# Attention forward on one core: the last head's two query halves in one PSUM tile or in two

## The chip, the cores and the metric

The kernel runs on one core of one Trainium2 chip. The metric is device microseconds of one execution. The kernel before takes 118.95 us, the median of three runs (118.91 to 118.98). One more execution was recorded by the profiler; its numbers are in the profile section below.

## The reference: what is computed

Softmax attention for 8 batches of 8 heads, 512 queries and 512 keys of 64 elements each, in float32, with no mask:

```python
def reference(q, k, v):
    scale = 1.0 / np.sqrt(q.shape[-1])
    scores = np.einsum('bhqd,bhkd->bhqk', q, k) * scale
    scores = scores - scores.max(axis=-1, keepdims=True)
    attn = np.exp(scores)
    attn = attn / attn.sum(axis=-1, keepdims=True)
    return np.einsum('bhqk,bhkd->bhqd', attn, v).astype(np.float32)
```

The kernel leaves the subtraction of the maximum out, since exp(x)/sum(exp(x)) is the same without it. It gets the sum of each row for nothing by giving V a 65th column of ones.

## The kernel before, in words

**Tiles.** The 64 heads are taken as 32 pairs (0 to 31). 512 queries and 512 keys are four chunks of 128 each. For every pair, q and k are cast to fp16 on GpSimd, transposed on TensorE into PSUM and copied to SBUF on VectorE. For every key chunk c and head h, TensorE then makes a block of scores with the 128 keys on the partitions and the 512 queries along the free dimension (L511). Two such blocks make a group, which fills one PSUM tile of the pool `ps_st`, tag `st`, of 128 x 2 x 512 float32. The pool holds three of these tiles and hands them out in turn: this is the score ring. One instruction on ScalarE exponentiates a whole group into an fp16 tile `pt` in SBUF (L516). Ten of the groups are exponentiated by VectorE instead (L533, L550).

**Values.** For one head and one chunk of 128 queries, four products (one for each key chunk c) accumulate 128 x 65 float32 in PSUM: `pt` is the stationary side and V with its ones column the moving side (L585). VectorE divides by the 65th column (L563, L565) into an SBUF ring, and SyncE stores a head when it is complete (L574).

**Who sets the order.** The class `Plan` steps through the kernel with costs written by hand and notes which step each engine takes next; the kernel then issues its instructions in that order. The engines wait for one another through semaphores, which a tile framework puts in by tile: an instruction that writes a tile waits for the earlier ones that read it, whichever part of the tile they touch.

**The last head.** The very last head (pair 31, h = 1) is not in the normal list (`Plan.last`). Its key chunks 0 and 1 are group 126. Its key chunks 2 and 3 are exponentiated in two half groups, 127 for queries 0 to 255 and 128 for queries 256 to 511 (`half` in `scores`, L489 to L517). So the last three tiles of the score ring are those of groups 126, 127 and 128. The values of this head are made by `last_values` in four parts (L593 to L609), from one more tile of the score ring, `o_last`, which follows group 128 and so takes the buffer of group 126:

- part 0: key chunk 0, all four query chunks (4 products), after the exponential of group 126
- part 1: key chunk 1, all four query chunks (4 products)
- part 2: key chunks 2 and 3, query chunks 0 and 1 (4 products), after the exponential of group 127
- part 3: key chunks 2 and 3, query chunks 2 and 3 (4 products), after the exponential of group 128

Query chunks 0 and 1 accumulate in `o[:, 0]`, query chunks 2 and 3 in `o[:, 1]` of the same tile. `finish` (L611 to L624) follows part 2 with the first half and part 3 with the second: a reciprocal on VectorE (L616), a multiplication on VectorE (L617), and a store of 64 KB, the first from SyncE's queue and the second from ScalarE's (L624).

In `Plan`, `wants` (L193) gives the exponential that each part needs, and `last_values` (L206) lets a part start when that exponential and the buffer are there.

Of the kernel before, what the change touches and what calls it, by code (L numbers as in the profile page):

```python
# [8 lines left out]
FP32 = mybir.dt.float32  # L9
# [8 lines left out]
class Plan:  # L18
# [174 lines left out]
    def wants(self, g, h, part):  # L193
        members = [self.member[(g, c, h)] for c in range(4)]
        if (g, h) == self.last:
            end = len(self.groups)
            members = [(members[0], members[1], end - 2, end - 1)[part]]
        exps = max(self.exps.get(m, 1e9) for m in members)
        return max(exps, self.cast_done.get((g, "v"), 1e9))

# [4 lines left out]

    def last_values(self, t):  # L206
        g, h = self.last
        if self.m < len(self.groups) or self.last_part == 4 or t < self.read[-3]:
            return False
        if t < self.wants(g, h, self.last_part):  # L210
            return False
        self.note(t, "last", self.last_part)
        self.full(t, self.V_UNIT)
        if self.last_part > 1:
            self.ready.append((self.pe + self.TO_DVE, "finish", (self.last_part,)))
        self.last_part += 1
        return True

# [124 lines left out]
def kernel(  # L343
# [7 lines left out]
    nc = tc.nc  # L351
    B, H, S, D = q.shape
    P = 128
    NI = S // P
# [4 lines left out]
    LAST = NP - 1  # L359
# [19 lines left out]
    opool = ctx.enter_context(tc.tile_pool(name="out", bufs=4))  # L379
    ps_st = ctx.enter_context(tc.tile_pool(name="ps_st", bufs=3, space=bass.MemoryType.PSUM))  # L380
# [16 lines left out]
    blocks = {}  # L397
# [4 lines left out]
    last = {}  # L402

    def source(src, g):
        b, h = g // ppb, 2 * (g % ppb)
        return src[b, h : h + 2].rearrange("h (p i) d -> p h i d", i=NI)
# [184 lines left out]
            )  # L591

    def last_values(part):  # L593
        if part == 0:
            o = ps_st.tile([P, 2, S], FP32, tag="st", name="o_last")
            last["o"] = [
                o[:, n, 0 : 2 * (D + 1)].rearrange("p (x d) -> p x d", x=2) for n in range(2)
            ]
        o = last["o"]
        for c in (part,) if part < 2 else (2, 3):  # L600
            for x in (range(NI), range(NI), (0, 1), (2, 3))[part]:
                nc.tensor.matmul(
                    o[x // 2][:, x % 2, :],
                    blocks[(LAST, c, 1)][:, x * P : (x + 1) * P],
                    vps[LAST % NV][:, 1, c, :],
                    start=(c == 0 and x % 2 == 0),
                    stop=(c == NI - 1),
                    skip_group_check=True,
                )  # L609

    def finish(part):  # L611
        o = last["o"][part - 2]
        n = slice(2 * part - 4, 2 * part - 2)
        ob = opool.tile([P, 2, D], FP32, tag="obl", name=f"obl_{part}")
        rc = opool.tile([P, 7, 1], FP32, tag="rc", name=f"rc_last_{part}")
        nc.vector.reciprocal(out=rc[:, 0:2], in_=o[:, :, D : D + 1])  # L616
        nc.vector.tensor_tensor(  # L617
            out=ob[:, :, :],
            in0=o[:, :, 0:D],
            in1=rc[:, 0:2].broadcast_to([P, 2, D]),  # L620
            op=AluOp.mult,
        )
        queue = (nc.sync, nc.scalar)[part - 2]
        queue.dma_start(out=source(out, LAST)[:, 1, n], in_=ob[:, :, :])  # L624

    def first_loads():
# [99 lines left out]
    with tc.manual_schedule():  # L726
        plan = Plan(groups, NP, 3)
        steps = plan.run()
        first_loads()
        for g, name in plan.first_loads:  # L730
            load(g, name)
        make_identity(nc, ident)
        nc.vector.memset(lift, LIFT[0])
        for p in (32, 96):
            nc.vector.memset(lift[p : p + 32], LIFT[1])
        for n in range(NV):
            nc.vector.memset(vps[n][:, :, :, D : D + 1], 1.0)
        first_pair()
        do = {
            "transposes": transposes,  # L740
            "scores": scores,
            "values": values,
            "load": load,
            "cast": cast_behind,
            "raise": raise_,
            "copy": lambda g, b: copy(g),
            "pass": pass_,
            "last": last_values,
            "finish": finish,
            "norm": lambda u, n, b: normalise(u, n),  # L750
        }
        for what, *args in steps:
            do[what](*args)
# [30 lines left out]
```

## Time and profile before

| what | value |
|---|---|
| three runs | 118.91, 118.95, 118.98 us |
| the profiled execution | 119.28 us |
| its span, first to last instruction | 117.5 us |
| outside the span (119.28 - 117.5) | 1.8 us |
| granted TensorE clock over the span | 1.000 |
| ScalarE busy | 110.7 us (94%), 123 instructions |
| TensorE busy | 105.0 us (89%), 1579 matmuls |
| VectorE busy | 98.2 us (84%), 174 instructions |
| 16 matmuls of the last head (L602) | 190 to 203 ns each, from 112.9 to 114.3 us |
| last reciprocals (L616), multiplications (L617) | 171 ns and 292 ns each, two of each |
| the two last stores (L624), issue to landing | 1.6 us each |

Times inside the profile are counted from the first instruction. The page gives for each engine its busy time, then the chain of work that ended last, then the costliest groups of instructions. The trace behind it answers with more: the chain in order of time, the instructions of an engine in order of time, the waits (who waited for whom, in total, times, longest), and the busy time of each engine in chosen stretches. "L602" is line 602 of the kernel; "PEld" is the load of the stationary side, "PE" the matmul itself, "q" behind an engine is its sequencer, which issues DMAs.

### The profile page before, as it was taken

The page shows a single profiled execution, that of the slowest core. Times are in us where ns is not written, and L with a number is a line of the kernel's source. Part 1 is how long each engine was busy: PE and PEld are TensorE (multiplying, and loading weights), DVE is VectorE, ACT ScalarE, POOL GpSimd, SP SyncE. Part 2 cuts the span into 40 slices and gives each one's busy share as a digit, 9 for nine tenths or more (in the row PEclk, how much of TensorE's full clock was granted, in tenths as well). Part 3 has the DMA queues.
Part 4 walks back from the last instruction along what each step waited for, and adds up shares of the span by engine and source line. Part 5 has one row for each costly group of instructions (what it writes and reads, how often), then busy time and mean ns, then how long its engine had stood idle before and what let it go on. Part 6 is the DMA issues. An engine that isn't in the chain of part 4 may idle for free.

```text
span 117.5 us, 4082 instructions
## 1 busy us (share of the span) xinstructions
PE 105.0 (89%) x1579; PEld 66.5 (57%) x1579; DVE 98.2 (84%) x174; ACT 110.7 (94%) x123; POOL 58.4 (50%) x102
## 2 busy tenths in 40 slices
PE   7969996987998999898997999999899998999970
PEld 2536653664655666355764575565566556666550
DVE  3463898699899999999999969899978999996371
ACT  4599999999999999999999999999999999999970
POOL 2388725944725843355583595569246553441000
PEclk9999999999999999999999999999999999999999
DMA  4999999999999999999899897999999993242353
GB/s 102 315 354 381 388 374 370 367 367 340 337 342 316 352 363 319 274 356 359 265 301 302 226 316 251 287 347 320 320 368 352 345 342 109 90 137 90 103 173 95
DMA packets 35604, 33.83 MB, mean 288 GB/s; under 512 B 2688, under 2 KB 35584, under 8 KB 35584
## 3 DMA queue, kind: packets, MB, share of 16 engines
q1 hardware_dynamic: 35152, 33.24, 86.0%
q10 hardware_dynamic: 432, 0.33, 0.9%
q8 instruction: 12, 0.20, 0.7%
q14 instruction: 8, 0.07, 0.2%
HBM read 25.17 MB, written 8.39 MB: 286 GB/s over the span
## 4 chain that ended last, share of the span: by engine, by line
ACT 44%; PE 24%; issue 12%; DVE 11%; POOL 3%; DMA 3%; SPq 1%; POOLq 0%; ACTq 0%
ACT pt L516 43%; PE st L511 8%; PE o L585 8%; DVE y L550 3%; PE st_0a L635 3%; DMA out_dram<-ring 3%; DVE z L533 2%; POOL qkp L445 2%; PE tp L469 2%; DVE ring L565 2%; DVE tqk L482 2%; DVE pd L550 1%; ACT pt L685 1%; PE st L678 1%; PE st L497 1%
## 5 line engine op out<-in xcount | busy, mean ns | idle before, releaser
L516 ACT ACTIVATE pt<-st 128x1024 f16<-128x1024 f32 (+1 forms) x116 | 105.7, 1293 | 0.0
L511 PE MATMUL st<-tqk 64*128 64x512 f16 (+1 forms) x250 | 45.6, 380 | 5.3 <-ACT pt L516 3.5
L585 PE MATMUL o<-vp,pt 128*128 128x65 f16 x928 | 42.3, 194 | 0.4 <-DVE tqk L482 0.2
L585 PEld LDWEIGHTS <-pt 128*128 128x128 f16 x928 | 35.6, 98 | 12.1 <-issue 10.9
L435 POOL CAST vp<-v 128x512 f16<-128x512 f32 x32 | 20.3, 640 | 16.4 <-DVE y L550 7.6
L445 POOL CAST qkp<-k 128x512 f16<-128x512 f32 x31 | 19.1, 615 | 14.7 <-DVE rc L563 2.6
L445 POOL CAST qkp<-q 128x512 f16<-128x512 f32 x30 | 18.5, 615 | 13.7 <-DVE pd L550 5.4
L565 DVE TENSOR_TENSOR ring<-o,rc 128x448 f32<-128x448 f32 (+2 forms) x37 | 22.6, 612 | 1.5 <-DVE rc L563 0.3
L511 PEld LDWEIGHTS <-tqk 64*128 64x128 f16 x250 | 13.1, 93 | 18.2 <-issue 10.4
L482 DVE COPY tqk<-tp 128x1024 f16<-128x1024 f16 x30 | 20.5, 684 | 1.0 <-PE tp L469 1.0
L469 PE MATMUL tp<-ident,qkp 128*128 128x128 f16 x248 | 19.6, 220 | 1.3 <-DVE tqk L482 0.6
L469 PEld LDWEIGHTS <-qkp 128*128 128x128 f16 x248 | 14.2, 97 | 9.5 <-issue 4.4
L533 DVE TENSOR_SCALAR z<-st 128x1024 f32<-128x1024 f32 x10 | 12.2, 1221 | 2.5 <-PE st L511 2.3
L563 DVE RECIPROCAL rc<-o 128x7 f32<-128x7 f32 (+2 forms) x37 | 7.4, 200 | 6.9 <-PE o L585 6.5
L550 DVE SCALAR_TENSOR_TENSOR y<-y 128x1024 f32<-128x1024 f32 x10 | 12.4, 1240 | 0.0
L550 DVE SCALAR_TENSOR_TENSOR y<-z 128x1024 f32<-128x1024 uint16 x10 | 12.3, 1234 | 0.1
L550 DVE SCALAR_TENSOR_TENSOR pd<-y,z 128x1024 uint32<-128x1024 f32 x10 | 12.2, 1217 | 0.0
L585 PE MATMUL o<-vp,pd 128*128 128x65 f16 x80 | 11.8, 195 | 0.0
L585 PEld LDWEIGHTS <-pd 128*128 128x128 f16 x80 | 7.8, 98 | 1.5 <-issue 0.8
L497 PE MATMUL st<-const-bfloat16-1.0,lift 64*128 64x512 bf16 x20 | 3.9, 380 | 0.8 <-ACT pt L516 0.6
L635 PE MATMUL st_0a<-const-bfloat16-1.0 128*128 128x512 bf16 (+1 forms) x11 | 3.5, 484 | 0.8 <-PEq L768 0.8
L635 PEld LDWEIGHTS <-const-bfloat16-1.0 128*128 128x128 bf16 x15 | 1.7, 131 | 2.4 <-issue 2.4
(48 smaller groups left out, 22.5 us busy)
## 6 DMA issues: line engine op xcount, KB each, us to landing
out_dram<-ring SPq DMA_DIRECT2D x63, 128.0 KB, 4.1
k<-in_k_dram SPq DMA_DIRECT2D x31, 256.0 KB, 5.1
q<-in_q_dram SPq DMA_DIRECT2D x31, 256.0 KB, 5.0
v<-in_v_dram SPq DMA_DIRECT2D x27, 256.0 KB, 5.0
v<-in_v_dram SPq DMA_DIRECT2D x10, 128.0 KB, 4.2
k<-in_k_dram ACTq DMA_DIRECT2D x2, 128.0 KB, 2.8
q<-in_q_dram SPq DMA_DIRECT2D x2, 128.0 KB, 2.7
out_dram<-obl SPq DMA_DIRECT2D x1, 64.0 KB, 1.6
```

Of the source, the lines that this page charges most:

```text
L435: return nc.gpsimd.tensor_copy(out=vps[g % NV][:, :, :, 0:D], in_=raw[g]["v"][:, :, :, :])
L445: return nc.gpsimd.tensor_copy(out=dst, in_=src[:, :, :, :])
L469: nc.tensor.transpose(tps[g][:, n, i, :], qkp[g][:, n, i, :], ident)
L482: nc.vector.tensor_copy(out=tqk[g][:, :, :], in_=tps.pop(g).rearrange("p n i c -> p n (i c)"))
L511: nc.tensor.matmul(st[:, x, cols], kc, qc[:, cols], start=not on_dve, stop=True)
L516: nc.scalar.activation(out=pt[:, :, cols], in_=st[:, :, cols], func=EXP, scale=scale)
L533: nc.vector.tensor_scalar(out=r["z"][:, :, :], in0=r["st"][:, :, :], scalar1=STEP, scalar2=2.0**17, op0=AluOp.mult, op1=AluOp.max,)
L550: nc.vector.scalar_tensor_tensor(out=r["bits"][:, :, :] if last else r["y"][:, :, :], in0=r["y"][:, :, :] if s else f, scalar=QUARTIC[s], ...
L563: nc.vector.reciprocal(out=rc[:, 0:n], in_=o[:, x : x + n, D : D + 1])
L565: nc.vector.tensor_tensor(out=ring[:, u % NU : u % NU + n, :], in0=o[:, x : x + n, 0:D], in1=rc[:, 0:n].broadcast_to([P, n, D]), op=AluOp. ...
L585: nc.tensor.matmul(os[u // 7][:, u % 7, :], blocks[(g, c, h)][:, y * P : (y + 1) * P], vps[g % NV][:, h, c, :], start=(c == 0), stop=(c == ...
L635: nc.tensor.matmul(dst[:, 0:n], ones[:, 0:P], ones[:, 0:n], start=True, stop=True)
```

## The change

The last head's two query halves get a tile of the score ring each, `o_last0` and `o_last1`, instead of two regions of one tile. Each tile is allocated when its half begins, so `o_last0` takes the buffer of group 126 and `o_last1` that of group 127. The four parts are now:

- part 0: key chunks 0 and 1, query chunks 0 and 1 (4 products), after the exponential of group 126
- part 1: key chunks 2 and 3, query chunks 0 and 1 (4 products), after that of group 127; the first `finish` follows
- part 2: key chunks 0 and 1, query chunks 2 and 3 (4 products), into the second tile
- part 3: key chunks 2 and 3, query chunks 2 and 3 (4 products), after the exponential of group 128; the second `finish` follows

The sixteen products, the reciprocals, multiplications and stores are the same instructions as before. The diff, cut to its core:

```diff
@@ Plan.wants
-            members = [(members[0], members[1], end - 2, end - 1)[part]]
+            members = [(members[1], end - 2, members[1], end - 1)[part]]
@@ Plan.last_values
-        if self.m < len(self.groups) or self.last_part == 4 or t < self.read[-3]:
+        if self.m < len(self.groups) or self.last_part == 4:
             return False
-        if t < self.wants(g, h, self.last_part):
+        if t < max(self.wants(g, h, self.last_part), self.read[self.last_part // 2 - 3]):
             return False
...
-        if self.last_part > 1:
-            self.ready.append((self.pe + self.TO_DVE, "finish", (self.last_part,)))
+        if self.last_part % 2:
+            self.ready.append((self.pe + self.TO_DVE, "finish", (self.last_part // 2,)))
@@ last_values
-        if part == 0:
-            o = ps_st.tile([P, 2, S], FP32, tag="st", name="o_last")
-            last["o"] = [
-                o[:, n, 0 : 2 * (D + 1)].rearrange("p (x d) -> p x d", x=2) for n in range(2)
-            ]
-        o = last["o"]
-        for c in (part,) if part < 2 else (2, 3):
-            for x in (range(NI), range(NI), (0, 1), (2, 3))[part]:
+        half, second = divmod(part, 2)
+        if not second:
+            o = ps_st.tile([P, 2, S], FP32, tag="st", name=f"o_last{half}")
+            last[half] = o[:, 0, 0 : 2 * (D + 1)].rearrange("p (x d) -> p x d", x=2)
+        for c in (2 * second, 2 * second + 1):
+            for x in range(2):
+                y = 2 * half + x
                 nc.tensor.matmul(
-                    o[x // 2][:, x % 2, :],
-                    blocks[(LAST, c, 1)][:, x * P : (x + 1) * P],
+                    last[half][:, x, :],
+                    blocks[(LAST, c, 1)][:, y * P : (y + 1) * P],
                     vps[LAST % NV][:, 1, c, :],
-                    start=(c == 0 and x % 2 == 0),
+                    start=(c == 0 and x == 0),
@@ finish
-    def finish(part):
-        o = last["o"][part - 2]
-        n = slice(2 * part - 4, 2 * part - 2)
+    def finish(half):
+        o = last[half]
+        n = slice(2 * half, 2 * half + 2)
...
-        queue = (nc.sync, nc.scalar)[part - 2]
+        queue = (nc.sync, nc.scalar)[half]
```

More of the change, by code (lines that the diff above doesn't have):

```diff
@@ L609, in last_values @@
                 )
-    def finish(part):
-        o = last["o"][part - 2]
-        n = slice(2 * part - 4, 2 * part - 2)
-        ob = opool.tile([P, 2, D], FP32, tag="obl", name=f"obl_{part}")
-        rc = opool.tile([P, 7, 1], FP32, tag="rc", name=f"rc_last_{part}")
+    def finish(half):
+        o = last[half]
+        n = slice(2 * half, 2 * half + 2)
+        ob = opool.tile([P, 2, D], FP32, tag="obl", name=f"obl_{half}")
+        rc = opool.tile([P, 7, 1], FP32, tag="rc", name=f"rc_last_{half}")
         nc.vector.reciprocal(out=rc[:, 0:2], in_=o[:, :, D : D + 1])
```

## The prediction, as it was put on record before the result

> **What bounds the kernel now.** First view: the page's opening line and, from its chain of work that ended last, the shares of the span by engine.
>
> ```profile
> span 117.5 us, 4082 instructions
> ...
> ACT 44%; PE 24%; issue 12%; DVE 11%; POOL 3%; DMA 3%; SPq 1%; POOLq 0%; ACTq 0%
> ```
>
> ScalarE has the largest share of the chain and is busy for 110.7 us: its exponentials set the pace up to the last of them. The change leaves them alone: in the two built programs every engine's instructions follow each other in the same order up to the sixteen products of the last head, and on ScalarE, VectorE, GpSimd and SyncE to the end. So only what comes after the last exponentials can move, and the second view is the chain in order of time over the last 5 us (start, length, what).
>
> ```profile
> 113.36 0.31 PE o_last L602 x4
> 113.68 0.02 issue
> 113.70 0.18 DVE rc_last L616
> 113.88 0.02 issue
> 113.91 0.30 DVE obl L617
> 114.21 0.04 issue
> 114.25 0.30 PE o_last L602 x4
> 114.55 0.02 issue
> 114.57 0.18 DVE rc_last L616
> 114.75 0.02 issue
> 114.78 0.29 DVE obl L617
> ```
>
> Read it as a zigzag. The exponential of group 127 ends at 113.31 and stands just ahead of these lines. Then come four products (part 2), the first half's reciprocal and multiplication on VectorE, and only then the last four products (part 3) and the second half's VectorE work. The exponential of group 128 is not in this chain: ScalarE's timeline has the last three exponentials end at 113.80 (111.30 + 2.50). The third view, the waits of the last microseconds (in total, times, longest), names what holds part 3.
>
> ```profile
> PE o_last L602 <- DVE obl L617: 0.6, 1, 0.6
> ```
>
> The fourth, the timeline, shows the same wait at the instructions, and the stores that close the kernel.
>
> ```profile
> 113.85 0.10 PEld L602 LDWEIGHTS <-pt 128*128 128x128 f16 x1 [0.31 <-ACT pt L516]
> ...
> 114.25 0.28 PE L602 MATMUL o_last<-vp,pt 128*128 128x65 f16 x4 [0.59 <-DVE obl L617]
> 114.26 0.40 SPq L624 DMA_DIRECT2D out_dram<-obl  x1
> ...
> 115.10 0.35 ACTq L624 DMA_DIRECT2D out_dram<-obl  x1
> ```
>
> The weights of part 3's first product were loaded at 113.85, 0.05 after the exponential of group 128; the product itself stood until 114.25, because it writes the tile that L617 was still reading. The two touch different columns of that tile; it is one tile in the program, and that is all that binds them. The last store (ScalarE's queue) is issued at 115.10, 0.03 after the last multiplication, and lands 1.55 later, at 116.65 (the trace's landing time); 0.84 of closing work follows to the end of the span.
>
> **The change, part by part.**
>
> *The wait that goes.* With two tiles part 3 no longer waits for L617. In the changed program its first product has no wait on VectorE left, and its first weight load still waits for the exponential of group 128. So part 3 starts at 113.85. Its length comes from the same four products after the other exponential: from the weight load at 113.36 to the reciprocal at 113.70 is 0.34. The second reciprocal can then start at 113.85 + 0.34 = 114.19 instead of 114.57: **0.38 earlier**.
>
> *What is late next.* VectorE must be free: the first multiplication runs from 113.91 to 114.20. In this trace an instruction of VectorE follows the one before it at anything from 0.08 before its reported end (wait met early, as in most of the L550 and L482 pairs) to 0.04 after it (the L616 to L617 step above). That puts the second reciprocal between 114.12 and 114.24; the products allow 114.19. So the gain lies between 0.33 (114.24) and 0.38, and I take 0.38, since a wait met by 114.19 is met before 114.20. The Trainium skill (VectorE: DVE Perf Modes, The DRAIN you can't avoid) says that the next instruction does not start until the pipe is empty; by that the start would be 114.20 and the gain 0.37. The overlaps of 0.08 in this trace speak against it.
>
> *The products that move.* Four products (key chunks 0 and 1, queries 256 to 511) go from before the exponential of group 127, where TensorE sat idle until 113.36, to right after part 1. Eight products issued together took 0.42 (112.87 to 113.29) against 0.30 for four, so they add 0.12 and are issued by about 113.63. Part 3 is due at 113.85: 0.22 to spare, cost nothing. If that cover were gone, part 3 would be late by at most 0.12. The first half (part 1) has the same four products behind the same exponential as before, so the first reciprocal stays at 113.70 and SyncE's store at 114.26.
>
> *The waits that come.* The second tile takes the buffer of group 127, which the exponential of group 127 reads. That exponential (ended 113.31) is what part 1 waits for anyway. The first product of part 2 gets one wait in the built program, on TensorE's own count up to the scores of group 127, which were made at 111.77 to 112.16: met long before. Should it nevertheless wait for part 1's products to be written (113.66, plus the 0.04 that a reciprocal needs behind them), part 2 would issue from 113.70 to 113.83, still before 113.85. So 0 to 0, and queued behind it is part 3 alone.
>
> *The last store.* VectorE's two instructions and the steps between them took 115.10 - 114.57 = 0.53 to the issue; so ScalarE's store is issued at 114.19 + 0.53 = 114.72. ScalarE has nothing else queued there. SyncE's issue lasts from 114.26 to 114.66, 0.06 before. What the 16 DMA engines do then is in the fifth view, stretches of the last 2 us (length, engines, clock, DMA share, GB/s).
>
> ```profile
> 115.25:115.53 0.28, 0.00 (x0) 0.00 (x0) 0.00 (x0) 0.00 (x0) 0.00 (x0) 1.00 0.65 185
> 115.53:115.95 0.42, 0.00 (x0) 0.00 (x0) 0.00 (x0) 0.00 (x0) 0.00 (x0) 1.00 0.00 0
> 115.95:116.32 0.37, 0.00 (x0) 0.00 (x0) 0.00 (x0) 0.00 (x0) 0.00 (x0) 1.00 0.61 177
> ```
>
> SyncE's store ends by 115.53, then the engines idle 0.42, then the last store runs 0.37. Moved by 0.38, the last store begins at 115.57, just behind. If it were to queue strictly behind SyncE's it could not begin before 115.53, so the gap caps any gain at 0.42.
>
> *Sum.* 0.38, from 119.28 to 118.90 for the profiled execution. Applied to the median of the runs shown, which is 0.33 below the profiled one: 118.95 - 0.38 = **118.57 us**. What the measurement of this kernel can tell from no change is about 0.2%, here 0.24.
>
> **The rivals.**
>
> *A. The second tile comes free only with the exponential of group 128.* Then eight products follow 113.85 instead of four: 0.12 later, gain 0.26, 118.69. Against it: the changed program has no such wait, and the buffers of the ring follow each other. Chance 0.07.
>
> *B. The two last stores get in each other's way.* They are now issued 0.06 apart instead of 0.44. SyncE's stores of 128 KB just before, each queued behind another, landed 1.8 to 1.9 after their issue instead of 1.55. With 1.86 the gain falls to 0.38 - 0.31 = 0.07: 118.88, within 0.2%. Against it: the transfers themselves do not overlap by the view above. The Trainium skill (Perfetto Trace Analysis, DMA Instruction — HWDGE) says that a sequencer locks the descriptor generator for its own use while it issues; by that ScalarE's issue would wait until 114.66, which is before 114.72, and nothing is lost. Chance 0.06.
>
> *C. The change does not do what it says,* or the end hangs on something else than this chain: 118.95. For it: 94% of the span is ScalarE's. Against it: SyncE's final wait ends 0.02 after the last store lands and nothing else is left. Chance 0.07.
>
> *D, slower: the last store meets a load of instructions.* The two stores that SyncE issued from 109.01 on (L574) landed 2.5 after their issue although the DMA engines were busy for 0.20 of 109 to 110; in that stretch the trace has single packets of the instruction queues, 8 to 16 KB, that hold one engine for 0.5 to 1.1. If the last store drew one, it would land after about 2.45, and the end would move by -0.38 + (2.45 - 1.55) = +0.52: 119.47. It turns into a loss where the landing takes over 1.55 + 0.38 = 1.93. Against it: the last such packet ends at 110.63, and the changed program has as many instructions as this one. Chance 0.06.
>
> **How the numbers follow.** The forecast has 0.74, A 0.07, B 0.06, C 0.07, D 0.06. Forecast and A are faster by over 0.2%: 0.81. B and C are the same: 0.13. D is slower: 0.06. The range: the largest gain is the 0.42 of the stores' gap (118.53), the smallest with the forecast and A is 0.26 (118.69); the runs spread by 0.07 and two medians are compared, so 0.08 below and 0.11 above: 118.45 to 118.80. It holds the forecast and A, 0.81.
>
> **What would show it.** Right: no wait of L601's products on L616 (the new numbers of these lines), part 3 issued at 0.05 after the last exponential, the second reciprocal starting within 0.05 of the end of the first multiplication, VectorE with no gap in its last four instructions after 113.70, ScalarE's store 0.38 earlier against the last exponential, and landing 1.55 after its issue. Wrong: a gap between the first multiplication and the second reciprocal (A), a landing over 1.7 (B, D), or a last exponential that itself ends elsewhere than 113.80, which nothing in the change explains.

## The result, and the profile after

The changed kernel takes 118.62 us against 119.12 us, medians of 22 runs each: ratio 0.996, 95% interval 0.9946 to 0.9973, which is 0.32 to 0.64 us less. The runs are much wider apart than the three shown before the prediction (118.91 to 118.98): 118.50 to 119.63 for the kernel before, 118.12 to 119.17 for the changed one. Two further measurements of the changed kernel gave 0.9989 and 0.9952 (below). All runs of both kernels together, 41 and 110, have means of 118.68 and 119.09: 0.42 less, with a 95% interval of 0.32 to 0.52. The 110 include 35 from a series that has no run of the changed kernel; the other series, each compared within itself and weighted by its runs, give 0.39.

The profiled execution took 118.68 us, with a span of 116.9. Its chain of work that ended last, in order of time (start, length, what), has lost the zigzag:

```profile
113.16 0.31 PE o_last L601 x4
113.47 0.02 issue
113.49 0.18 DVE rc_last L615
113.67 0.02 issue
113.70 0.29 DVE obl L616
113.99 0.18 DVE rc_last L615
114.17 0.02 issue
114.19 0.29 DVE obl L616
```

The second reciprocal now follows the first multiplication without a step back to TensorE. The waits of the last microseconds (in total, times, longest) no longer have a wait for that multiplication; what is left before the last head's products is a wait for exponentials:

```profile
PEld L601 <- ACT pt L516: 0.5, 2, 0.3
DVE rc L563 <- PE o L585: 0.3, 1, 0.3
PE o_last L601 <- ACT pt L516: 0.2, 1, 0.2
```

And the timeline shows the last exponential, the products and the stores:

```profile
112.55 1.05 ACT L516 ACTIVATE pt<-st 128x512 f16<-128x512 f32 x1
...
113.64 0.18 PEld L601 LDWEIGHTS <-pt 128*128 128x128 f16 x4 [0.19 <-ACT pt L516]
113.70 0.29 DVE L616 TENSOR_TENSOR obl<-o_last,rc_last 128x128 f32<-128x128 f32 x1
113.98 0.17 DVE L615 RECIPROCAL rc_last<-o_last 128x2 f32<-128x2 f32 x1
114.05 0.40 SPq L623 DMA_DIRECT2D out_dram<-obl  x1
...
114.51 0.35 ACTq L623 DMA_DIRECT2D out_dram<-obl  x1
```

The weights of part 3 are now loaded four in a row at 113.64, where the kernel before loaded one and stood.

The spans of the two profiled executions differ by 0.6, and that is not the gain. The last exponential ended at 113.59 in this execution (112.55 and 1.05 long, with rounding) and at 113.80 in the execution before:

```profile
112.75 1.05 ACT L516 ACTIVATE pt<-st 128x512 f16<-128x512 f32 x1
```

That 0.21 lies ahead of anything that the change touches: 0.09 of it is there at the first exponential, and the rest builds up evenly over the kernel. In the eleven profiled executions of this study the last exponential ended anywhere from 113.32 to 114.25. So the tail is read from the end of the last exponential, and every run below is read so, too:

| from the end of the last exponential, us | before | after |
|---|---|---|
| first reciprocal starts | -0.10 | -0.10 |
| first multiplication ends | 0.40 | 0.40 |
| part 3's first product starts | 0.45 | 0.06 |
| second reciprocal starts | 0.77 | 0.39 |
| last store issued | 1.30 | 0.92 |
| last store landed | 2.85 | 2.47 |
| end of the span | 3.69 | 3.31 |

0.38 is gained in one place, at part 3's start (0.39) and the second reciprocal's (0.38), and is carried unchanged to the end. The packets of the last store begin 0.06 after the last of SyncE's and take 0.36 (stretches: length, engines, clock, DMA share, GB/s):

```profile
115.31:115.37 0.06, 0.00 (x0) 0.00 (x0) 0.00 (x0) 0.00 (x0) 0.00 (x0) 1.00 0.03 9
115.37:115.73 0.36, 0.00 (x0) 0.00 (x0) 0.00 (x0) 0.00 (x0) 0.00 (x0) 1.00 0.62 181
```

### The profile page after: what moved, and what is told of

It reads as the page before. It is cut to its first block, busy times and chain, and to the rows that moved or that the text cites. A ratio compares the mean times of both kernels' runs of the same rounds, so it can differ in the third digit from the quotient of the medians.

```text
span 116.9 us, 4082 instructions
## 1 busy us (share of the span) xinstructions
PE 105.0 (90%) x1579; PEld 66.4 (57%) x1579; DVE 98.1 (84%) x174; ACT 110.6 (95%) x123; POOL 57.9 (50%) x102
## 4 chain that ended last, share of the span: by engine, by line
ACT 52%; PE 25%; DVE 11%; issue 9%; ACTq 0%
ACT pt L516 50%; PE st L511 9%; PE o L585 9%; DVE y L550 3%; PE st_0a L634 3%; PE tp L469 2%; ACT pt L684 2%; DVE z L533 2%; DVE tqk L482 2%; DVE ring L565 2%; DVE pd L550 1%; PE st L497 1%; DVE rc L563 1%; DVE obl L616 0%; DVE rc_last L615 0%
## 5 line engine op out<-in xcount | busy, mean ns | idle before, releaser
L435 POOL CAST vp<-v 128x512 f16<-128x512 f32 x32 | 19.6, 616 | 15.4 <-DVE y L550 7.6
```

Of the source, the lines that this page charges most:

```text
L435: return nc.gpsimd.tensor_copy(out=vps[g % NV][:, :, :, 0:D], in_=raw[g]["v"][:, :, :, :])
```

## The experiments

Theory W is the prediction's: what cost the time was part 3's wait for the first half's multiplication, and nothing else of the change matters. Rival O puts the gain down to the new order of the products, rival P to the two separate buffers.

### Two tiles and the new order, with the wait put back

```diff
@@ last_values
-                nc.tensor.matmul(
+                product = nc.tensor.matmul(
...
+                if (part, c, x) == (3, 2, 0):
+                    tc.add_manual_dep(product.ins, last["mult"].ins.name, SYNC, reason="first half")
@@ finish
-        nc.vector.tensor_tensor(
+        last["mult"] = nc.vector.tensor_tensor(
```

> The changed kernel with one wait added: the first product of part 3 (key chunk 2, query chunk 2) waits again until the first half's multiplication is done; two tiles and the new order of products stay. Measured from the end of the last exponential: the second reciprocal started 0.77 us after it in the kernel before and 0.39 us after it in the changed one, and the last store landed 2.85 and 2.47 us after it. Theory W (the wait on the first half's multiplication was the whole loss): 0.77 and 2.85 again, the time of the kernel before within 0.2%. Rival O (the new order of the products brings the gain, since the first half's four early products no longer stand beside the second half's): 0.39 and 2.47 stay, about 0.4 us faster than before. Rival P (two separate buffers let VectorE read and TensorE write without meeting): also 0.39 and 2.47.

Measured: the second reciprocal starts 0.87 after the last exponential, the last store lands 2.95 after it; 119.02 us, ratio to before 1.000 (0.9975 to 1.0025). Everything that the change gained is gone, with both tiles and the new order in place. Rivals O and P fall: neither the order nor the two buffers bring anything while the wait stands. Whether the two halves could also run at once within one tile is not shown; no run takes the wait away there. Theory W had 0.77 and 2.85; the timeline shows where the further 0.10 is:

```profile
113.53 0.29 DVE L618 TENSOR_TENSOR obl<-o_last,rc_last 128x128 f32<-128x128 f32 x1
113.89 0.41 SPq L625 DMA_DIRECT2D out_dram<-obl  x1
113.94 0.19 PEld L601 LDWEIGHTS <-pt 128*128 128x128 f16 x4 [0.65 <-ACT pt L516]
113.97 0.29 PE L601 MATMUL o_last<-vp,pt 128*128 128x65 f16 x4 [0.56 <-DVE obl L618]
```

Here the wait stands ahead of the weight load; in the kernel before it stood on the product, behind a weight load that was already done. The multiplication ended at 113.83, the weight load began 0.11 later and the product 0.15 later, against 0.05 in the kernel before.

### Two tiles, the old order

```diff
@@ Plan.wants
-            members = [(members[1], end - 2, members[1], end - 1)[part]]
+            members = [(members[0], members[1], end - 2, end - 1)[part]]
...
@@ last_values
-        half, second = divmod(part, 2)
-        if not second:
-            o = ps_st.tile([P, 2, S], FP32, tag="st", name=f"o_last{half}")
-            last[half] = o[:, 0, 0 : 2 * (D + 1)].rearrange("p (x d) -> p x d", x=2)
-        for c in (2 * second, 2 * second + 1):
-            for x in range(2):
+        if part == 0:
+            for n in range(2):
+                o = ps_st.tile([P, 2, S], FP32, tag="st", name=f"o_last{n}")
+                last[n] = o[:, 0, 0 : 2 * (D + 1)].rearrange("p (x d) -> p x d", x=2)
+        for c in (part,) if part < 2 else (2, 3):
+            for x in (range(NI), range(NI), (0, 1), (2, 3))[part]:
...
```

> Two tiles alone: the order of the products is that of the kernel before (key chunk 0 for all four query chunks, then key chunk 1, then part 2, part 3). The second tile's buffer comes free with the exponential of group 127, so two products run early and ten follow that exponential instead of four. Theory W: part 3 is not held, but the first reciprocal comes about six products (0.19 us) later, so VectorE is busy with the first half until about 0.58 us after the last exponential and the second reciprocal starts at 0.50 to 0.58; the last store lands 2.58 to 2.66 after it, 0.19 to 0.27 us faster than before. Rival O: as slow as before, 0.77 and 2.85. Rival P: as the changed kernel, 0.39 and 2.47.

Measured: second reciprocal at 0.48, last landing at 2.55; 118.84 us, ratio 0.9984 (0.9960 to 1.0008). By the profile it keeps 0.30 of the 0.38; the whole runs cannot tell that from nothing. The chain in order of time:

```profile
113.17 0.48 PE o_last L600 x10
113.66 0.02 issue
113.68 0.18 DVE rc_last L614
113.86 0.02 issue
113.88 0.29 DVE obl L615
114.17 0.09 DVE rc_last L614
```

The "x10" in the first line are the ten products that now stand behind the exponential of group 127. They make the first half late, and VectorE itself is what the second half waits for: the products of part 3 were there at 0.35, the reciprocal had to wait for its engine. It began 0.08 before the reported end of the multiplication ahead of it (0.483 against 0.565). Theory W put it at 0.50 to 0.58 and the landing at 2.58 to 2.66; both came 0.02 to 0.03 under these ranges. So removing the wait is the gain, and the new order lets the last 0.08 of it through.

### One tile, the new order

```diff
@@ last_values
-        if not second:
-            o = ps_st.tile([P, 2, S], FP32, tag="st", name=f"o_last{half}")
-            last[half] = o[:, 0, 0 : 2 * (D + 1)].rearrange("p (x d) -> p x d", x=2)
+        if part == 0:
+            o = ps_st.tile([P, 2, S], FP32, tag="st", name="o_last")
+            for n in range(2):
+                last[n] = o[:, n, 0 : 2 * (D + 1)].rearrange("p (x d) -> p x d", x=2)
```

> The new order alone: both halves in one tile, as in the kernel before. Part 2 is issued before the first half's VectorE work and into the same tile, so the first reciprocal waits for eight products after the exponential of group 127 instead of four (0.12 us later), and part 3 waits for the first multiplication as before. Theory W: second reciprocal 0.89 us after the last exponential, last store landed 2.97 after it, 0.12 us slower than before (0.1%, hardly beyond what the runs can tell; the profile shows it). Rival O: 0.39 and 2.47. Rival P: 0.77 to 0.89, as theory W.

Measured: 0.90 and 2.97, as theory W has it; 119.36 us, ratio 1.0014 (0.9992 to 1.0037). The new order alone is 0.12 worse than the kernel before by the profile. The waits name the same culprit as in the kernel before, and a second one, the first reciprocal behind eight products:

```profile
PE o_last L602 <- DVE obl L617: 0.6, 1, 0.6
DVE rc_last L616 <- PE o_last L602: 0.5, 2, 0.4
```

Of the 0.5 in the second line, 0.15 is the first reciprocal's and new; the other 0.37 is the second reciprocal's and stands in the kernel before, too.

### The last store: split, without its neighbour, on one queue

The last store was the prediction's rivals B and D. Three kernels change only the stores. First, the last one cut in two:

```diff
@@ finish
-        queue = (nc.sync, nc.scalar)[half]
-        queue.dma_start(out=source(out, LAST)[:, 1, n], in_=ob[:, :, :])
+        if half:
+            for x, queue in enumerate((nc.scalar, nc.sync)):
+                s = slice(64 * x, 64 * x + 64)
+                queue.dma_start(out=source(out, LAST)[s, 1, n], in_=ob[s])
+        else:
+            nc.sync.dma_start(out=source(out, LAST)[:, 1, n], in_=ob[:, :, :])
```

> The changed kernel with the last store cut in two by partitions: 0 to 63 from ScalarE's queue, 64 to 127 from SyncE's, 32 KB each, both released by the last multiplication. The store of 64 KB landed 1.55 us after its issue, of which its packets took 0.36. If the two queues issue side by side, the packets of each half are through in about 0.2 and the later one lands about 1.4 after the multiplication, 0.1 to 0.2 us better than the changed kernel. If one queue's issue has to wait for the other's (an issue takes 0.35), the later half is issued 0.35 later and lands about 0.2 us worse.

Measured: 119.60 us, ratio to before 1.0039 (1.0019 to 1.0059): slower than the kernel before, though all up to the issue is as in the changed one (second reciprocal at 0.39, issue at 0.92). The halves land at 2.76 and 3.03. In the timeline the two issues overlap and take 0.54 and 0.55, where one alone takes 0.35 to 0.40:

```profile
114.86 0.54 ACTq L625 DMA_DIRECT2D out_dram<-obl  x1
114.90 0.55 SPq L625 DMA_DIRECT2D out_dram<-obl  x1
```

The packets came late and in turn: ScalarE's from 1.20 after its issue (0.85 for the store of 64 KB in the kernel before), SyncE's when ScalarE's were nearly through. The issues did not come strictly one after the other, as my second case had it, but neither did they run side by side at the length of one alone; the cost of 0.56 is nearly three times what I allowed. The Trainium skill (Perfetto Trace Analysis, DMA Instruction — HWDGE) has one descriptor generator that a sequencer locks for its own use until its descriptors are made. If that took the whole issue, the first of the two would not grow and the second would end about an issue's length behind it; the trace does not agree, since both grew alike and ended 0.04 apart.

What the 0.56 comes from stays open. This run cuts the store in two and makes two issues overlap, and no run does one without the other. An overlap alone need not lengthen issues so much. The timeline of the kernel before starts with loads of 128 KB from the same two queues, two from each, all but at the same time:

```profile
0.73 0.89 ACTq L630 DMA_DIRECT2D k<-in_k_dram  x2
0.74 0.84 SPq L631 DMA_DIRECT2D q<-in_q_dram  x2
```

These are loads and not stores, but they take at most 0.45 an issue on average, and the split-store kernel's own first loads take the same (0.89 and 0.86 for two).

Second, no store of the first half, whose rows stay unwritten:

```diff
@@ finish
-        queue.dma_start(out=source(out, LAST)[:, 1, n], in_=ob[:, :, :])
+        if half:
+            queue.dma_start(out=source(out, LAST)[:, 1, n], in_=ob[:, :, :])
```

> The changed kernel without the store of the first half (queries 0 to 255 of the last head are not written). In the changed kernel SyncE's issue of that store ends 0.07 us before ScalarE's issue of the last one begins, and its packets end 0.06 before the last store's begin. If the two stores do not meet (the forecast), the last one is issued 0.92 us after the last exponential, lands 1.55 after that, 2.47 in all, as in the changed kernel. If they already meet (rival B), it lands sooner, by up to the 0.1 us by which packets or descriptors are held.

Measured: issue at 0.92, landing 1.55 later, 2.47 in all, in one run of 119.40 us (its last exponential ended late, at 114.25). By this profile the last store of the changed kernel loses nothing to its neighbour.

Third, both on SyncE's queue:

```diff
@@ finish
-        queue = (nc.sync, nc.scalar)[half]
+        queue = nc.sync
```

> The changed kernel with both last stores on SyncE's queue. SyncE's issue of the first ends 0.86 us after the last exponential and it needs about 0.09 between two issues, so the second is issued at 0.95 instead of 0.92 and, with the 1.55 to 1.61 of the two last stores so far, lands 2.50 to 2.56 after the last exponential: 0.03 to 0.09 worse than the changed kernel, within 0.2% by the time. If two queues were what keeps the stores apart, it is worse by 0.35 or more, as in the split store.

Measured: second issue at 0.95, landing at 2.55; 118.69 us, ratio 0.9982 (0.9964 to 1.0000). 0.07 worse than the changed kernel by the profile, within the range expected. By whole runs it comes out 0.23 faster than the changed kernel of the same series (118.92, next section), the other way round: single series of ten runs do not resolve such steps. One queue after itself costs little: 0.09 between the two issues.

### The changed kernel again, and the kernel before against itself

The runs spread more than I had counted on, so I measured the size itself again.

> The changed kernel once more, beside the others on one chip: by the forecast 0.38 us faster than before (ratio 0.9968), 2.47 us from the last exponential to the last landing. The first measurement gave 0.996 (0.9946 to 0.9973); if that held something besides the wait, the ratio stays at 0.9955 or less while the profile still shows 2.47.

Measured: 118.92 us, ratio 0.9989 (0.9971 to 1.0008). The profile shows the same tail, 0.39 and 2.48. That is neither the 0.9968 of the forecast, which lies just below this interval, nor the alternative's "0.9955 or less". In a further series both kernels were timed side by side:

> The kernel before, unchanged, timed against itself beside the changed kernel: ratio 1.000, and its interval shows what a comparison of this size can tell. If it comes out 0.001 or more away from 1, the 0.9989 of the second measurement of the changed kernel and the 0.996 of the first differ by nothing but the spread of the runs.

Measured: 119.16 us, ratio 0.9996 (0.9976 to 1.0015). A comparison of this size tells 0.2% and no less. It came out 0.0004 from 1, not the 0.001 or more by which I would have put the difference between 0.9989 and 0.996 down to the spread of the runs alone; so this run does not settle that difference.

> The changed kernel a third time, beside the kernel before timed against itself. By the forecast 0.38 us faster (ratio 0.9968) and 2.47 us from the last exponential to the last landing. The two measurements so far give 0.996 and 0.9989; if the change loses part of its gain ahead of the last exponential, the ratio stays near 0.9985 with the same 2.47.

Measured, with seven runs: 118.37 us, ratio 0.9952 (0.9931 to 0.9972), and 0.39 and 2.48 in the profile. The three ratios, 0.996, 0.9989 and 0.9952, scatter around the forecast, and the five profiled tails of the two kernels (two of the kernel before, three of the changed one) repeat themselves within 0.01 up to the last landing. Nothing is lost or won ahead of the last exponential that these runs could show. Part of the scatter goes with the mean granted TensorE clock on record for the single runs (last section). In the second measurement 6 of 12 runs of the changed kernel were granted less than 0.995, against 6 of 23 of the kernel before; in the third it was none of 7 against 9 of 18. That mix pulls the two ratios apart in the way seen, but the runs at 0.998 or more still differ by 0.14 in the second (118.70 against 118.84) and by 0.42 in the third (118.40 against 118.81), five to six runs on the changed side; the rest of the scatter stays unexplained.

## Why the prediction was right, point by point

- **What bounds the end.** The zigzag between TensorE and VectorE was the chain, and putting the wait back took the whole gain away (and 0.10 more by the profile). Shown.
- **The wait that goes, 0.38.** Part 3 begins 0.05 after the last exponential with its weight load, as forecast, and the second reciprocal 0.39 after it (0.77 before): 0.38 by the profile. The time came out 0.50 lower by the first medians and 0.42 (0.32 to 0.52) over all runs; 0.38 lies in both intervals. So the mechanism and its size were right.
- **The total, 118.57 against 118.62.** That it agrees this closely is luck. The median of the kernel before was 119.12 in this measurement, 0.17 above the 118.95 that I subtracted from, and the medians differ by 0.50, 0.12 more than forecast; the two nearly cancel. The two other medians of the changed kernel, 118.92 (12 runs) and 118.37 (7 runs), lie outside the range of 118.45 to 118.80.
- **What is late next.** I took the products, not VectorE, to set the start of the second reciprocal. It started at 113.98, 0.04 after the last product's end and just before the first multiplication's. The forecast had 114.19 for the products and 114.12 to 114.24 for VectorE, so the choice between them was close. In the two-tile kernel with the old order VectorE did set it, and there the overlap of 0.08 is seen. The prediction named a rule of the Trainium skill (VectorE: DVE Perf Modes, The DRAIN you can't avoid) that the next instruction starts only when the pipe is empty. The same passage says that an instruction that is not held, which means that it need not wait until all earlier ones have finished, starts earlier; the prediction left that out. The two starts, 0.006 and 0.08 before the reported end of the instruction ahead, agree with that; whether the pipe is empty by the reported end, no view here shows.
- **The products that move.** Eight products were issued by 0.20 before the last exponential's end; the cover was 0.25, forecast 0.22. No run took this cover away. In the two-tile kernel with the old order part 3 still begins at 0.06; the 0.08 lost there is VectorE's, which is late with the first half.
- **The waits that come.** Nothing: part 2's first product followed part 1's last within 0.03.
- **The last store.** Issued 0.53 after the second reciprocal, landed 1.55 after that, as forecast; SyncE's store beside it costs it nothing (one profile without that store). Rivals B and D did not come about, A and C are refuted by the profile.
- **What was off.** The size of what can be told. I took the 0.07 between three runs as the spread and 0.2% as the limit; the runs spread by over 1 us, and the median of three of the 22 runs could have been anything from 118.24 to 118.98. I also named a last exponential that ends elsewhere than 113.80 as a sign of being wrong. It ended at 113.59, and in the two further profiles of the changed kernel at 113.90 and 113.43: it moves from execution to execution and says nothing about the change. Last, I called the gap between the two stores' packets (0.42) the cap of any gain and gave their issues no such limit. The issues were 0.07 apart after the change, so a gain of over 0.45 would have made them overlap, just behind that cap; no run comes near enough to show what either limit costs for whole stores.

## What to carry to other kernels

Where one engine stands until another has read a different part of the same tile, give each part its own tile, and order the work so that the first part is finished first; the tile alone kept 0.30 of 0.38 here, the order alone lost 0.12. Read such a tail from the last event that the change cannot touch: the profile then shows 0.38 to within 0.01, while whole runs need dozens to show it at all. Measure before splitting a closing store over two queues: it cost 0.56 here, and what part of that is the cut and what part the overlap of the two issues is not shown.

## What the runs showed of the hardware that was not expected

- A store of 64 KB cut in two halves, issued 0.04 apart from two queues, came out much slower than whole: the issues took 0.54 and 0.55 instead of 0.35 to 0.40, and the halves landed 1.84 and 2.08 after their issue instead of 1.55. Overlapping issues of 128 KB loads at the start of the kernel stay at 0.45 or less each on average.
- In one trace, a wait ahead of a weight load costs 0.10 more than the same wait on the product behind it: 0.15 against 0.05 from the release to the first product.
- The same kernel takes 118.94 us on average in the 46 runs of the kernel before with a mean granted clock of at least 0.998, and 119.33 in the 33 below 0.995 (of 88 whose clock is on record). Among the runs at 0.998 or more the changed kernel (30 of them) takes 118.57: 0.36 less, nearest to the profile's 0.38. The low mean is not slow TensorE work, as far as the traces show. The three traces with a mean below 0.995 (0.990 and 0.994, and 0.991 in the split store) have 1.00 in the stretch from 0 to 115.0, in which TensorE ends its last product, and 0.54, 0.72 and 0.63 after it. What makes those runs longer stays open.
